# A retrieval search in a decoder block: seven weight tiles asked for ahead instead of four, and expert numbers computed before their gate weights

## The chip, the cores and the metric

The kernel runs on one core of one Trainium2 chip. The metric is the device time of one execution in microseconds (us); lower is better. The core has TensorE (PE, with its weight loads shown apart as PEld), VectorE (DVE), ScalarE (ACT), GpSimd (POOL) and SyncE (SP), which here issues most of the weight loads. Each engine runs its own list of instructions in a fixed order and waits on semaphores for the others; the DMA queues do the same.

## The reference, cut to what matters

512 tokens of width 1024 pass three attention-like mixers with gates and an output projection (`x`), and then a retrieval of experts, `peer_ffn`:

```
q  = h @ w_q                                  # 8 heads, two halves of 128 each
s1 = q[..., 0, :] . keys1 ; s2 = q[..., 1, :] . keys2      # 128 scores per half
v1, i1 = top_k(s1, 16) ; v2, i2 = top_k(s2, 16)
sv, si = top_k(all sums v1 + v2, 16)
experts = i1[si // 16] * 128 + i2[si % 16]    # the expert numbers
gates   = softmax(sv)                         # the gate weights
a   = h . u[experts]                          # 128 rows of u for each token
out = (gelu(a) * gates) . v[experts]          # 128 rows of v for each token
```

`u` and `v` hold 16384 rows of 1024 floats. The arithmetic of the kernel is 32-bit.

## The kernel before, in words

The tokens form four blocks of 128. `mixers(0)` computes the mixers for block 0, and `mixers(1)` those for blocks 1 to 3 together. While `mixers(1)` runs, a generator called `beside()` weaves in block 0's retrieval: the search, the numbers and weights, and then the rows of `u` and `v` that block 0's tokens picked ("tokens in rows": each row is gathered by an indirect DMA on POOL and multiplied on DVE). A function `pump`, called at each weight load of `mixers(1)`, moves `beside()` on by some credit. Blocks 2 and 3 are later done with dense matrix products over all experts, and block 1 in rows again beside them.

The order of instructions on each engine up to the end of the second search is not the order of the code. A scheduler with its own model of time builds it when the kernel is compiled: any edit moves instructions on every engine behind it. After the second search the order of POOL, DVE and PE is that of the code.

What the change touches lies in `beside()`:

- `search` for block 0 has 16 products on PE (line 766: `mm<-aT,...`), one for each head and half, each with a query weight tile of 512 KB from `w_pq`. `fetch` gives each its buffer: three slices of the idle tensor `mg1` and one buffer `raw`, four in turn. A tile is asked for when the code comes to its product, and its DMA waits until the product that used the buffer before is over.
- Per head, PE then does the scores (line 774), ACT copies them (line 777), and DVE finds the top 16 (lines 731 to 735).
- `weigh` computes the gate weights: a difference on DVE (line 801, tile `ex`), an exponential on ACT (line 804), a sum, a reciprocal and a product on DVE (810, 811, 813, tile `gate`).
- `numbers_of` computes the expert numbers `eidx` (DVE, up to line 869) and the tokens times norm factors, `h2n`, in tile `own` (DVE, line 872). Each gather (line 908) needs `eidx`, each row product (line 929, `scr<-row,own`) needs a landed row and `own`.

Other names in the rows: `rsy` (POOL, line 210) is the power -1/2 behind the norm of attention heads and waits for DVE's `rsv` (line 209), which needs DVE's sums of squares `hss` (line 351), which need ACT's squares of a finished PE product (line 350). `wlo` (DVE, line 138) is the low part of a weight tile that is split in two for exactness; PE's products of `mixers(1)` (lines 152 to 154) need it. `w_skvf`, `w_nat`, `w_o` and `w_out` are weights of the mixers. `qT`, `ohi` and `olo` are buffers of the attention: its queries, and the high and low part of its output.

## Time and profile before

| | us |
|---|---|
| median of 3 runs | 1552.13 |
| the runs | 1544.93, 1552.13, 1552.81 |
| the profiled execution, its own time | 1548.8 |
| its span (first to last instruction) | 1547.0 |
| PE busy | 1498.3 (97%) |
| DVE busy | 1419.4 (92%) |
| ACT busy | 812.4 (53%) |
| POOL busy | 778.1 (50%) |

The span is the profiler's, from the first to the last instruction, and 1.8 us lie around it. Block 0's search stands between 177 and 221 us of the span; its rows and `mixers(1)` fill the time to about 640 us; the second search ends near 760 us. Matmuls are pipelined and their ends are modelled, so the busy time of PE in a stretch is an upper bound of its work.

### The profile page before, as it was taken

How to read it: one execution, taken by the hardware profiler on the slowest of the kernel's cores; microseconds unless marked ns; L12 is line 12 of the kernel's file. 1: busy time of each engine (PE TensorE's matmuls, PEld its weight loads, DVE VectorE, ACT ScalarE, POOL GpSimd, SP SyncE). 2: the span in 40 equal slices, each digit the busy share in tenths (PEclk: the TensorE clock that was granted, in tenths of full speed). 3: DMA queues.
4: the chain of work that ended last, by engine and by line, in shares of the span. 5: the costliest groups of instructions: out<-in, count | busy, mean ns of one | idle time of the engine just before them, and what ended most of it. 6: DMA issues, size and time to landing. Idle time of an engine off the chain costs nothing.

```text
span 1547.0 us, 27092 instructions
## 1 busy us (share of the span) xinstructions
PE 1498.3 (97%) x9411; PEld 1360.5 (88%) x9411; DVE 1419.4 (92%) x2673; ACT 812.4 (53%) x1806; POOL 778.1 (50%) x642
## 2 busy tenths in 40 slices
PE   8999999999999989999999999999999999999998
PEld 7999899997897989999888887788888888888887
DVE  6689488989999999999999999899999999999998
ACT  7778346646345533352225899545444544544543
POOL 1101016767667456877445666545554544555451
PEclk9999999999998999999999999999999999999999
DMA  8688657998999898986998999999999999999995
GB/s 325 207 289 300 246 174 280 338 362 302 360 367 325 293 356 317 352 310 232 327 365 329 393 395 384 373 397 398 401 410 403 408 410 404 411 410 410 410 410 209
DMA packets 180125, 533.48 MB, mean 345 GB/s; under 512 B 17660, under 2 KB 48148, under 8 KB 179988
## 3 DMA queue, kind: packets, MB, share of 16 engines
q0 software_dynamic: 73728, 268.47, 45.9%
q1 hardware_dynamic: 96180, 227.54, 40.1%
q10 hardware_dynamic: 10080, 35.75, 5.8%
q8 instruction: 74, 1.21, 0.3%
q14 instruction: 63, 0.52, 0.1%
HBM read 516.99 MB, written 14.69 MB: 344 GB/s over the span
## 4 chain that ended last, share of the span: by engine, by line
PE 52%; issue 14%; DMA 11%; POOL 9%; DVE 9%; ACT 4%; POOLq 0%; DVEq 0%; SPq 0%; ACTq 0%
PE mm L153 9%; PE mm L152 9%; PE mm L154 9%; POOL row L908 9%; PE mm L1078 5%; DMA row<-in_peer_v_dram,eidx 4%; DMA row<-in_peer_u_dram,eidx 3%; PE sc L1078 3%; DVE wlo L138 2%; DMA gd<-st 2%; PE mm L766 2%; DVE o L1144 2%; DVE scr L929 1%; PE tp L384 1%; PE sc L506 1%
## 5 line engine op out<-in xcount | busy, mean ns | idle before, releaser
L908 POOL DMA_INDIRECT row<-in_peer_v_dram,eidx x256 | 322.2, 1258 | 298.3 <-DVE two L942 175.5
L908 POOL DMA_INDIRECT row<-in_peer_u_dram,eidx x256 | 315.4, 1232 | 219.8 <-DVE scr L929 115.8
L138 DVE TENSOR_TENSOR wlo<-raw,whi 128x1024 fp32r<-128x1024 f32 (+1 forms) x228 | 277.2, 1220 | 21.7 <-ACT whi L123 17.5
L942 DVE SCALAR_TENSOR_TENSOR two<-row,acts,two 128x1024 f32<-128x1024 f32 x197 | 252.6, 1282 | 5.3 <-DMA row<-in_peer_v_dram,eidx 3.1
L123 ACT CAST whi<-raw 128x1024 fp32r<-128x1024 f32 x146 | 152.2, 1050 | 119.2 <-PE mm L153 75.4
L929 DVE SCALAR_TENSOR_TENSOR scr<-row,own 128x1024 bf16<-128x1024 f32 x128 | 156.2, 1220 | 7.1 <-DMA row<-in_peer_u_dram,eidx 6.4
L929 DVE SCALAR_TENSOR_TENSOR scr<-row,two 128x1024 bf16<-128x1024 f32 x115 | 139.5, 1213 | 3.8 <-DMA row<-in_peer_u_dram,eidx 2.9
L210 POOL TENSOR_TENSOR rsy<-rsv,mhalf 128x4 f32<-128x4 f32 (+5 forms) x25 | 37.8, 1515 | 177.2 <-DVE rsv L209 176.3
L1212 ACT CAST ah<-ga 128x256 fp32r<-128x256 f32 x116 | 47.1, 407 | 150.2 <-PE tp L153 125.0
L152 PE MATMUL mm<-hhi,whi 128*128 128x384 f32 x320 | 110.8, 346 | 1.8 <-ACT hhi L244 1.4
L153 PE MATMUL mm<-hlo,whi 128*128 128x384 f32 x320 | 110.7, 346 | 0.0
L154 PE MATMUL mm<-hhi,wlo 128*128 128x384 f32 x320 | 109.9, 343 | 0.0
L152 PE MATMUL mm<-whi,hhi 128*128 128x256 f32 (+1 forms) x360 | 103.6, 290 | 2.7 <-ACT hhi L681 1.9
L1214 ACT CAST whi<-raw 128x1024 fp32r<-128x1024 f32 x96 | 100.3, 1047 | 9.5 <-DMA raw<-in_peer_v_dram 4.6
L153 PE MATMUL mm<-wlo,hhi 128*128 128x256 f32 (+1 forms) x360 | 102.7, 286 | 1.3 <-DVE wlo L138 1.3
L153 PE MATMUL sc<-wlo,ah 128*128 128x512 f32 x256 | 101.2, 395 | 2.5 <-DVE wlo L138 2.5
L152 PE MATMUL sc<-whi,ah 128*128 128x512 f32 x256 | 100.8, 394 | 1.3 <-ACT whi L1214 1.2
L154 PE MATMUL mm<-whi,hlo 128*128 128x256 f32 (+1 forms) x360 | 102.0, 285 | 0.0
L154 PE MATMUL sc<-whi,al 128*128 128x512 f32 x256 | 101.2, 395 | 0.0
L153 PE MATMUL tp<-wlo,ah 128*128 128x512 f32 x256 | 101.1, 395 | 0.0
L152 PE MATMUL tp<-whi,ah 128*128 128x512 f32 x256 | 101.0, 395 | 0.0
L154 PE MATMUL tp<-whi,al 128*128 128x512 f32 x256 | 100.6, 393 | 0.0
(332 smaller groups left out, 4478.2 us busy)
## 6 DMA issues: line engine op xcount, KB each, us to landing
raw<-in_peer_v_dram SPq DMA_DIRECT2D x96, 512.0 KB
hhi<-in_uT_dram ACTq DMA_DIRECT2D x68, 512.0 KB
raw<-in_w_tr_dram SPq DMA_DIRECT2D x48, 512.0 KB
raw<-in_w_nat_dram SPq DMA_DIRECT2D x40, 512.0 KB
last<-in_peer_v_dram SPq DMA_DIRECT2D x32, 512.0 KB
hhi<-in_uT_dram SPq DMA_DIRECT2D x26, 512.0 KB
raw<-in_w_o_dram SPq DMA_DIRECT2D x24, 512.0 KB
gd<-st SPq DMA_DIRECT2D x24, 512.0 KB
```

The lines of the kernel that those rows point to most:

```text
L123: ins = (cast or A.copy)(hi[:, :n * w], raw[:, :n * w])
L138: V.tensor_sub(lo, raw, hi.bitcast(F32))
L152: PE.matmul(ps, lh, rh, start=first, stop=False)
L153: PE.matmul(ps, lh, rl, start=False, stop=False)
L154: PE.matmul(ps, ll, rh, start=False, stop=last)
L210: G.tensor_tensor(y, v, mhalf[:, :n], op=OP.pow)
L908: ins = G.indirect_dma_start(out=r, out_offset=None, in_=t["peer_" + tab], in_offset=bass.IndirectOffsetOnAxis(ap=eidx[b][:, j:j + 1], axi ...
L929: V.scalar_tensor_tensor(scr, r, 1.0, two[0] if b else h2n[b], op0=OP.mult, op1=OP.mult, accum_out=acts[b][:, c]))
L942: V.scalar_tensor_tensor(two[0], r, acts[b][:, c], two[0], op0=OP.mult, op1=OP.add))
L1078: PE.matmul(ps[:, :TD], w[:, dc], h2f[dc], start=dc == 0, stop=dc == KC - 1)
L1212: A.copy(ah, a)
L1214: A.copy(hi, raw)
```

## The change

`fetch` now has seven buffers: to the three slices of `mg1` and `raw` come the buffers `qT`, `ohi` and `olo`, which nothing uses between the end of `mixers(0)` and the first queries and outputs of `mixers(1)`. It asks for tile i+6 when tile i is taken, so seven are asked for at the start. And `numbers_of` now comes ahead of `weigh`; two orders are pinned with `follow` (an edge for the scheduler without a semaphore): `own` and the first difference of the weights stand behind the cast to `eidx` on DVE.

```diff
-    def weigh(pool, f, g):
+    def follow(ins, after):
+        if after:
+            tc.add_manual_dep(ins.ins, after[-1], mybir.DependencyInfo(
+                mybir.DependencyClass.NoSync, mybir.DependencyReason.DATA), reason="behind the numbers")
+
+    def weigh(pool, f, g, after=()):
...
-        V.tensor_sub(ex, f.best, f.best[:, :, :, 0:1].to_broadcast([128, nb, PH, TOPK]))
+        follow(V.tensor_sub(ex, f.best, f.best[:, :, :, 0:1].to_broadcast([128, nb, PH, TOPK])), after)
...
-    def numbers_of(pool, f, lb, b, iota_k):
+    def numbers_of(pool, f, lb, b, iota_k, done=None):
...
-        V.tensor_copy(eidx[b], e[0])
+        ins = V.tensor_copy(eidx[b], e[0])
+        if done is not None:
+            done.append(ins.ins.name)
...
-        V.scalar_tensor_tensor(h2n[b], x1[b], rstd[:, b:b + 1], g2r, op0=OP.mult, op1=OP.mult)
+        follow(V.scalar_tensor_tensor(h2n[b], x1[b], rstd[:, b:b + 1], g2r, op0=OP.mult, op1=OP.mult), done)
...
-            lent, turns = by_token(wide("mg1", BIG)), [0]
+            lent = by_token(wide("mg1", BIG))
+            slots = [lent[:, i] for i in range(BIG)] + [qq.tile([128, D], F32, tag="raw", name="raw", bufs=1)]
+            slots += [pp.tile([128, 4, BIG * 128], F32, tag=tag, name="raw", bufs=1).rearrange("p a b -> p (a b)")[:, :D]
+                      for tag in ("qT", "ohi", "olo")]
+            asked, taken = [0], [0]
 
             def fetch(src, n):
-                i = turns[0] % (BIG + 1)
-                turns[0] += 1
-                raw = lent[:, i] if i < BIG else qq.tile([128, D], F32, tag="raw", name="raw", bufs=1)
-                fill(raw, src, n)
-                return raw
+                i = taken[0]
+                taken[0] += 1
+                while asked[0] < min(i + len(slots), 2 * PH):
+                    fill(slots[asked[0] % len(slots)], t["w_pq"][asked[0]], n)
+                    asked[0] += 1
+                return slots[i % len(slots)]
...
-            yield from weigh(pool, f, 0)
-            yield from numbers_of(pool, f, 0, 0, iota_k)
+            numbered = []
+            yield from numbers_of(pool, f, 0, 0, iota_k, numbered)
+            yield from weigh(pool, f, 0, numbered)
```

Three places of the compiled order bear on the prediction. In the rows a name is a tile, `<-` its sources, and xN counts equal rows; the changed kernel's lines stand 5 to 7 higher there (908 is 915, 929 is 936, 872 is 879).

The first is SP's list of loads around the start of the search, before (`mg1_2400` is `mg1`, `raw_2445` the buffer `raw`):

```order
L117 DMA raw_2340<-in_w_out_dram 128x1024
L117 DMA mg1_2400<-in_w_pq_dram 128x1024 x2
L117 DMA raw_2346<-in_w_out_dram 128x1024
L117 DMA mg1_2400<-in_w_pq_dram 128x1024
L758 DMA keys_2401<-in_keysT_dram 128x256
L758 DMA keys_2432<-in_keysT_dram 128x256
L117 DMA raw_2445<-in_w_pq_dram 128x1024
L117 DMA raw_2699<-in_w_skvf_dram 128x1056
L117 DMA raw_2891<-in_w_skvf_dram 128x1056
L117 DMA raw_3044<-in_w_nat_dram 128x1024
L117 DMA mg1_2400<-in_w_pq_dram 128x1024
```

The same stretch of SP now (`raw_2401` is the buffer `raw`, `raw_2403` lies in `ohi`, `raw_2404` in `olo`; the load into `qT` stands 13 rows further up, ahead of the last load of `w_o`):

```order
L117 DMA mg1_2400<-in_w_pq_dram 128x1024 x2
L117 DMA raw_2346<-in_w_out_dram 128x1024
L117 DMA mg1_2400<-in_w_pq_dram 128x1024
L117 DMA raw_2403<-in_w_pq_dram 128x1024
L117 DMA raw_2404<-in_w_pq_dram 128x1024
L758 DMA keys_2405<-in_keysT_dram 128x256
L117 DMA raw_2401<-in_w_pq_dram 128x1024
L758 DMA keys_2442<-in_keysT_dram 128x256
L117 DMA raw_2704<-in_w_skvf_dram 128x1056
L117 DMA raw_2885<-in_w_skvf_dram 128x1056
L117 DMA raw_3041<-in_w_nat_dram 128x1024
L117 DMA mg1_2400<-in_w_pq_dram 128x1024
```

Seven loads of `w_pq` now stand ahead of `w_skvf`, where four stood; the rows after the first four tiles alternate with `w_nat` as before.

The second is POOL's list from the first head norms of `mixers(1)`, before (`rsy` is the norm, `row` a gathered row of `u`):

```order
L210 TENSOR_TENSOR rsy<-rsv,mhalf 128x6
L210 TENSOR_TENSOR rsy<-rsv,mhalf 128x12
L908 DMA row<-in_peer_u_dram,eidx_212 128x1024 x6
L210 TENSOR_TENSOR rsy<-rsv,mhalf 128x12
L908 DMA row<-in_peer_u_dram,eidx_212 128x1024 x9
L210 TENSOR_TENSOR rsy<-rsv,mhalf 128x12
L908 DMA row<-in_peer_u_dram,eidx_212 128x1024 x7
```

And POOL now:

```order
L210 TENSOR_TENSOR rsy<-rsv,mhalf 128x6
L210 TENSOR_TENSOR rsy<-rsv,mhalf 128x12 x2
L915 DMA row<-in_peer_u_dram,eidx_212 128x1024 x14
L210 TENSOR_TENSOR rsy<-rsv,mhalf 128x12
L915 DMA row<-in_peer_u_dram,eidx_212 128x1024 x7
```

The second norm of 12 heads' sums has moved from behind the first six gathers to ahead of all of them.

The third is DVE's list from the last load split ahead of the first rows, before:

```order
L138 TENSOR_TENSOR wlo<-raw,whi 128x1024
L209 SCALAR_TENSOR_TENSOR rsv<-hss,eps 128x12
L929 SCALAR_TENSOR_TENSOR scr,acts_213<-row,own 128x1024 x2
L481 MEMSET qn 128x12
L483 TENSOR_SCALAR qn<-cum 128x12
L929 SCALAR_TENSOR_TENSOR scr,acts_213<-row,own 128x1024
L138 TENSOR_TENSOR wlo<-raw,whi 128x1024 x2
```

The cast to `eidx` stands five rows above this list: behind it came two pairs of `hss` and `wlo`, the second of which opens the list. The same place of DVE now (`own` and three of the four DVE instructions of the weights have come between the cast and this list, beside the two pairs):

```order
L138 TENSOR_TENSOR wlo<-raw,whi 128x1024
L209 SCALAR_TENSOR_TENSOR rsv<-hss,eps 128x12
L818 TENSOR_TENSOR gate_216<-ex,gden 128x8x16
L481 MEMSET qn 128x12
L483 TENSOR_SCALAR qn<-cum 128x12
L936 SCALAR_TENSOR_TENSOR scr,acts_213<-row,own 128x1024
L138 TENSOR_TENSOR wlo<-raw,whi 128x1024
L936 SCALAR_TENSOR_TENSOR scr,acts_213<-row,own 128x1024
```

The `wlo` that stood behind three rows stands behind one. On ACT the weights' exponential, which stood among the copies of the `w_skvf` product, now stands ahead of the last squares that this `rsv` needs, with a table load of its own; the later table load ahead of the attention's first exponential is gone.

## The prediction, and how it was worked out

> **What bounds the kernel now.** I read the page's shares and slices first, then the chain of work that ended last, then busy time by stage, and then the lists of PE, DVE, POOL and SP around block 0's search.

> ```profile
> span 1547.0 us, 27092 instructions
> PE 1498.3 (97%) x9411; PEld 1360.5 (88%) x9411; DVE 1419.4 (92%) x2673; ACT 812.4 (53%) x1806; POOL 778.1 (50%) x642
> PE 52%; issue 14%; DMA 11%; POOL 9%; DVE 9%; ACT 4%; POOLq 0%; DVEq 0%; SPq 0%; ACTq 0%
> 250.00:475.00 225.00, 220.68 (x1519) 201.88 (x1518) 208.82 (x392) 123.54 (x312) 159.69 (x120) 1.00 0.95 348
> 475.00:640.00 165.00, 152.78 (x956) 145.48 (x955) 157.80 (x213) 72.06 (x145) 105.39 (x76) 0.94 0.91 323
> 640.00:760.00 120.00, 120.00 (x672) 113.70 (x671) 119.39 (x623) 41.95 (x74) 84.83 (x87) 1.00 0.81 294
> ```

> PE and DVE share the bound; the last three rows give, after the length, the busy time of PE, PEld, DVE, ACT, POOL, then the granted clock. From 250 to 475 us DVE is idle 225 - 208.82 = 16.2 us and PE at most 4.3: there PE's stream leads and DVE has room. From 475 to 640 both have gaps (12.2 and 7.2 us) and the clock drops; from 640 to 760 DVE is full. So time saved on PE at 213 us can reach the end if PE stays ahead up to 640.

> The search itself is paced by PE, and PE waits in it for tiles:

> ```profile
> 177.08 0.39 PE L766 MATMUL mm<-aT,mg 128*128 128x128 f32 x2
> 188.71 3.84 PE L766 MATMUL mm<-aT,mg 128*128 128x128 f32 x32 [1.31 <-DMA mg<-in_w_pq_dram]
> 193.62 2.05 PE L766 MATMUL mm<-aT,raw 128*128 128x128 f32 x16 [1.07 <-DMA raw<-in_w_pq_dram]
> 195.51 0.61 PE L774 MATMUL sc<-keys,qp 128*128 128x128 f32 x4
> 196.31 0.91 PE L766 MATMUL mm<-aT,mg 128*128 128x128 f32 x6 [0.19 <-DMA mg<-in_w_pq_dram]
> 212.38 0.37 PE L152 MATMUL mm<-whi,hhi 128*128 128x264 f32 x1
> ```

> The brackets are the idle time ahead of a row and what ended it: 1.31 + 1.07 + 0.19 = 2.57 us in the 35.3 us from 177.08 to 212.38, where PE goes over to the mixers.

> **Part 1: seven tiles ahead.** No instruction is added; the 16 loads of 512 KB are issued earlier by SP.

> ```profile
> 158.85 0.42 SPq L117 DMA_DIRECT2D mg<-in_w_pq_dram  x1
> 172.41 0.42 SPq L117 DMA_DIRECT2D raw<-in_w_pq_dram  x1
> 180.96 0.33 SPq L117 DMA_DIRECT2D mg<-in_w_pq_dram  x1
> 161.45 3.72 PE L326 MATMUL mm<-raw,own 128*128 128x256 f32 x16 [0.33 <-ACT own L678]
> L153 PE MATMUL mm<-wlo,ohi x16: 275/279/283, 152.7 to 159.9; 128*128 128x256 f32 x16
> 162.00:171.00 9.00, 8.31 (x40) 7.09 (x39) 0.84 (x2) 1.61 (x5) 0.00 (x0) 1.00 0.25 102
> 177.00:192.00 15.00, 13.69 (x123) 13.50 (x122) 10.34 (x50) 6.99 (x18) 2.17 (x9) 1.00 0.85 314
> ```

> Before, three tiles are asked for by 158.85, the fourth at 172.41 and the fifth only at 180.96, when the first buffer is read. Now `ohi` and `olo` are free when PE's last product with them ends, about 160.2, and their loads stand ahead of the `keys` on SP, so they land in the stretch from 162 to 171, where the queues carry 102 GB/s (the last two figures of a row: share of the DMA engines, GB/s). `qT`'s load stands ahead of the last `w_o` and `w_out` loads on SP and delays each by its own length: at the 314 GB/s of 177 to 192, 0.52 MB take 1.7 us. The first `w_out` product (161.45) waits for ACT, not for its weights, so I cost that at nothing; if that cover were gone it costs up to 1.7.

> From the eighth tile on, a tile is asked for when PE leaves its buffer, about 181 for the first, and is needed seven products later. A product of 16 rows' matmuls takes 2.05 us by the row at 193.62, so that is 14 us, in which the queues move 4.4 MB at 314 GB/s: eight tiles' worth, for three or four tiles of `w_pq` and four of `w_nat` asked for meanwhile. So the 2.57 us go, whole; the bounds are 0 (the loads between eat the lead) and 2.57, and I take 2.57. PE then reaches `mixers(1)` at 209.8, and DVE, which waits for the scores, ends its search as much earlier.

> **Part 2: numbers before weights, on DVE.**

> ```profile
> 220.70 0.29 DVE L801 TENSOR_TENSOR ex<-best 128x128 f32<-128x128 f32 x1
> 223.10 0.28 DVE L810 TENSOR_REDUCE gden<-ex 128x8 f32<-128x128 f32 x1
> 223.77 0.19 DVE L811 RECIPROCAL gden<-gden 128x8 f32<-128x8 f32 x1
> 225.50 0.41 DVE L813 TENSOR_TENSOR gate<-ex,gden 128x128 f32<-128x128 f32 x1
> 225.82 1.28 DVE L872 SCALAR_TENSOR_TENSOR own<-mg,rstd,g2r 128x1024 f32<-128x1024 f32 x1
> 241.11 0.23 DVE L869 CAST eidx<-e 128x128 int32<-128x128 f32 x1
> 244.31 0.17 DVE L209 SCALAR_TENSOR_TENSOR rsv<-hss,eps 128x12 f32<-128x12 f32 x1
> 249.53 1.23 DVE L929 SCALAR_TENSOR_TENSOR scr<-row,own 128x1024 bf16<-128x1024 f32 x1 [5.06 <-DMA row<-in_peer_u_dram,eidx]
> 254.59 2.35 DVE L138 TENSOR_TENSOR wlo<-raw,whi 128x1024 fp32r<-128x1024 f32 x2
> ```

> Five instructions leave the way to `eidx`: 0.29 + 0.28 + 0.19 + 0.41 + 1.28 = 2.45 us, about 2 without the overlaps of neighbours. With part 1 the cast, 241.11 before, comes 2.57 + 2 = 4.5 us earlier, about 236.6. By itself that brings the gathers forward as much. But the order of POOL has changed too.

> ```profile
> 234.72 2.44 POOL L210 TENSOR_TENSOR rsy<-rsv,mhalf 128x12 f32<-128x12 f32 x1 [7.74 <-DVE rsv L209]
> 242.34 1.58 POOL L908 DMA_INDIRECT row<-in_peer_u_dram,eidx  x1 [5.18 <-ACT sq L350]
> 250.21 2.71 POOL L210 TENSOR_TENSOR rsy<-rsv,mhalf 128x12 f32<-128x12 f32 x1
> 221.34 0.40 ACT L804 ACTIVATE ex<-ex,rstd 128x128 f32<-128x128 f32 x1
> 224.17 1.28 ACT L439 ACT_TABLE_LOAD   x1
> 255.86 0.39 PE L153 MATMUL mm<-wlo,hhi 128*128 128x256 f32 x1 [1.28 <-DVE wlo L138]
> ```

> **Part 3: the gathers behind the second norm.** Before, `rsv` of 244.31 waits on POOL behind six gathers until 250.21. Now all gathers stand behind that norm. `rsv` hangs on PE's product and ACT's squares: 2.57 earlier at best, 241.7. Ahead of these squares ACT now has the weights' exponential and its table load, 0.40 + 1.28 = 1.7 us, so 243.4 at worst. The norm then takes 2.44 to 2.71 us with 0.2 ahead of and behind it: the first gather starts between 244.6 and 246.6, against 242.34. It comes 2.3 to 4.2 us later, though its numbers are 4.5 us earlier.

> DVE began the first row 249.53 - 242.34 = 7.2 us after its gather's start, so now at 251.8 to 253.8, and stands idle from about 242 on. Behind that row in its list stands the `wlo` for which PE waited 1.28 us before. It ends 1.23 + 1.2 us after the row's start, the 1.2 being half the pair of 2.35 at 254.59: 254.2 to 256.2, instead of 255.8. PE is ready for it at 255.86 - 1.28 - 2.57 = 252.0. So PE waits 2.2 to 4.2 us there, and goes on 1.7 us earlier to 0.3 later than before. I take the middle, 0.7 earlier: of 2.57 us gained in the search 1.9 go back. The terms in one line: -2.57 (tiles) + 1.9 (row and `wlo`) = -0.7.

> [...]

> The rows start 2.3 to 4.2 us later on DVE. I cost that at nothing behind this place: the 16.2 us idle on DVE up to 475 cover it, and the rows that stand ahead of the attention's later steps in DVE's list are fewer or the same. Without that cover it is up to 4.2 us in the full stretch up to 760. `weigh`'s last product on DVE (0.41) falls into the wait for the first row; the gate weights are read only after all 128 rows of `u`. The table load is one that stood later and goes there.

> The sum holds for the profiled execution: 1548.8 - 0.7 = 1548.1. That execution is 3.3 us under the median of the three runs, 1552.13, by which it would be 1551.4; I start from the middle of the two, 1550.5, and predict **1550**. The three runs differ by 7.9 us, 0.5%, which is about what a measurement of this kernel can tell from no change.

> **The rivals.** *PE's clock falls at the new wait (slower).* PE would stand 2.2 to 4.2 us in one piece. A wait like that has been seen in this trace:

> ```profile
> 482.67 0.44 PE L384 MATMUL tp<-cst,p 128*128 128x128 f32 x2 [2.12 <-ACT p L547]
> 480.00:485.00 5.00, 2.21 (x14) 1.74 (x13) 5.00 (x11) 3.30 (x9) 3.93 (x3) 0.87 1.00 354
> 485.00:490.00 5.00, 4.19 (x15) 3.02 (x15) 4.96 (x12) 2.45 (x7) 4.19 (x4) 0.50 0.94 308
> 490.00:495.00 5.00, 4.96 (x21) 4.24 (x20) 4.78 (x8) 1.90 (x4) 4.09 (x4) 0.61 0.87 300
> ```

> PE idled 2.8 of 5 us and ran at 0.50 and 0.61 afterwards: 0.13 x 5 + 0.50 x 5 + 0.39 x 5 = 5.1 us of lost clock. The shorter waits in the search left it at 1.00. From about 2.8 us of idle on it decides: -0.7 + 5.1 = +4.4, some 1555; with the wait at its upper bound and the late rows uncovered, 0.3 + 5.1 + 4.2 = +9.6, 1560. [...] Chance 0.22.

> *The order is kinder than I read it (faster).* The row lands sooner than 7.2 us, since weight loads share the queues less, and the gain of 2.57 stays; and the altered order around 480, with a row or two fewer ahead of the window attention's last steps in DVE's list, spares the clock drop there: -2.57 - 5.1 = -7.7, some 1543. That the gap at 480 is made of row products between short attention steps speaks for it; that as many matrix products as before are left to fill it speaks against. Chance 0.22.

> *The change doesn't do what it says.* SP's waits hold the extra loads back, or the queues do, and the search waits as before: then only part 3 is left, +1.9, some 1552. The idle queues from 162 to 171 speak against it. Chance 0.08.

> **How the numbers follow.** My forecast, a search without waits whose gain is mostly given back, has 0.48: 1547 to 1552 from the two starting points with its bounds. The range reaches to both clock cases, with the runs' own half spread of 4 us at each end cut to what leaves 2 in 10 out: 1541 to 1559. Faster by over 0.5% (under 1544.4) is most of the kind case and a share of the forecast through the runs' spread: 0.15 + 0.05 = 0.20. Slower by over 0.5% (over 1559.9) is the far end of the clock case and something not seen: 0.07 + 0.05 = 0.12. Within: 0.68.

> **What would show it.** Part 1: no idle time of PE for `w_pq` and a search of 32.7 us on PE. Part 2: `eidx` near 236.6. Part 3: the norm of 12 ahead of the first gather, that at 244.6 to 246.6, DVE idle 9 us or more for the first row, PE waiting for `wlo` near 252. The clock in 250 to 275 tells the slow rival, that in 480 to 495 the fast one. I am wrong if PE runs through 252 to 256, or if the stretches behind 475 differ by more than 5 us.

## The result, and the profile after

The changed kernel takes 1560.96 us (median of 8 runs, 1555.07 to 1566.08) against 1552.12 for the kernel before (8 runs beside it, 1544.93 to 1554.93): a ratio of 1.0060, with a 95% interval of 1.0039 to 1.0082. It is slower, by more than the prediction's range (1541 to 1559) allowed.

The page of the kernel after, its first two lines:

```profile
span 1558.2 us, 27098 instructions
PE 1504.3 (97%) x9411; PEld 1364.2 (88%) x9411; DVE 1418.9 (91%) x2673; ACT 812.5 (52%) x1806; POOL 782.3 (50%) x642
```

The span is 11.2 us longer with the same instructions on PE, DVE, ACT and POOL. PE is busy 6.0 us longer, which is about what the clock lost (44.4 us at half speed instead of 30.7, half of the difference is 6.8); the rest is waits. Busy time by stage, in the columns of the prediction's rows:

```profile
177.00:213.00 36.00, 36.00 (x315) 35.74 (x314) 24.09 (x150) 11.39 (x33) 5.38 (x25) 1.00 0.68 247
250.00:475.00 225.00, 221.40 (x1514) 202.93 (x1513) 202.68 (x382) 121.40 (x303) 161.85 (x119) 0.99 0.93 343
475.00:640.00 165.00, 148.32 (x929) 140.10 (x928) 153.37 (x204) 68.97 (x144) 98.68 (x72) 0.92 0.88 309
640.00:760.00 120.00, 118.31 (x679) 112.91 (x678) 116.52 (x627) 46.05 (x79) 88.38 (x90) 1.00 0.84 299
```

From 475 to 640 us PE's idle time has grown from 12.2 to 16.7 us, DVE's from 7.2 to 11.6, and the clock has gone from 0.94 to 0.92.

Setting the starts of the same PE products in the two traces against each other tells where PE falls behind. "Clock" is half of the time for which the granted clock stood at 0.5, against the kernel before.

| stretch (time of before), us | PE later by, us | of which clock |
|---|---|---|
| 150 to 177, ahead of the search | +1.6 | +1.7 |
| 177 to 212, the search | -3.3 | 0 |
| 212 to 262, start of `mixers(1)` | +5.4 | +1.7 |
| 262 to 470 | +0.6 | +1.7 |
| 470 to 642 | +7.8 | +3.4 |
| 642 to the end | -1.2 | 0 |

So the search gained what was predicted, and two places gave back four times as much: the start of `mixers(1)`, which the prediction worked out, and a stretch 260 us behind the edit, which it had costed at nothing. (The first row of the table is no work of the change; the last section says why.) PE's list in the kernel after, first the search, then its waits of 0.2 us or more up to 262 us:

```profile
179.04 0.39 PE L766 MATMUL mm<-aT,mg 128*128 128x128 f32 x2
208.62 2.17 PE L766 MATMUL mm<-aT,mg 128*128 128x128 f32 x18
210.55 0.37 PE L152 MATMUL mm<-whi,hhi 128*128 128x264 f32 x1
...
227.86 0.33 PE L377 MATMUL tg<-cst,qn 128*128 128x128 f32 x1 [1.79 <-ACT qn L363]
229.35 0.55 PE L152 MATMUL mm<-whi,hhi 128*128 128x256 f32 x1 [0.20 <-ACT sq L350]
247.62 0.39 PE L152 MATMUL mm<-whi,hhi 128*128 128x256 f32 x1 [0.63 <-ACT sq L350]
259.70 0.39 PE L153 MATMUL mm<-wlo,hhi 128*128 128x256 f32 x1 [0.44 <-DVE wlo L138]
```

No product from 179.04 to 210.55 waits for `w_pq`; the search takes 31.5 us instead of 35.3. The new wait stands at 227.86, and the one forecast near 252 is missing. POOL and DVE around it:

```profile
223.57 3.62 POOL L210 TENSOR_TENSOR rsy<-rsv,mhalf 128x6 f32<-128x6 f32 x1 [5.51 <-DVE rsv L209]
249.92 2.27 POOL L210 TENSOR_TENSOR rsy<-rsv,mhalf 128x12 f32<-128x12 f32 x1 [9.09 <-DVE rsv L209]
252.37 1.15 POOL L915 DMA_INDIRECT row<-in_peer_u_dram,eidx  x1 [0.18 <-PE tg L377]
...
229.23 0.07 DVE L487 MEMSET qn<- 128x12 f32 x1 [1.60 <-PE tg L377]
242.03 0.23 DVE L874 CAST eidx<-e 128x128 int32<-128x128 f32 x1
249.76 0.41 DVE L818 TENSOR_TENSOR gate<-ex,gden 128x128 f32<-128x128 f32 x1
257.27 1.23 DVE L936 SCALAR_TENSOR_TENSOR scr<-row,own 128x1024 bf16<-128x1024 f32 x1 [4.69 <-DMA row<-in_peer_u_dram,eidx]
```

The first row is the norm of 6 heads' sums, which took 1.78 us before:

```profile
225.20 1.78 POOL L210 TENSOR_TENSOR rsy<-rsv,mhalf 128x6 f32<-128x6 f32 x1 [6.53 <-DVE rsv L209]
```

The expert numbers are ready at 242.03, later than before (241.11), and the gathers start at 252.37 instead of 242.34.

### The profile page after: what moved, and what is told of

It reads as the page before. It is cut to its first block, busy times and chain, and to the rows that moved or that the text cites. A ratio compares the mean times of both kernels' runs of the same rounds, so it can differ in the third digit from the quotient of the medians.

```text
span 1558.2 us, 27098 instructions
## 1 busy us (share of the span) xinstructions
PE 1504.3 (97%) x9411; PEld 1364.2 (88%) x9411; DVE 1418.9 (91%) x2673; ACT 812.5 (52%) x1806; POOL 782.3 (50%) x642
## 4 chain that ended last, share of the span: by engine, by line
PE 47%; DVE 16%; issue 14%; POOL 10%; DMA 7%; ACT 5%; POOLq 0%; DVEq 0%; SPq 0%; another core or an unknown queue 0%; ACTq 0%
POOL row L915 8%; PE mm L154 7%; PE mm L153 7%; PE mm L152 7%; PE mm L1091 5%; PE sc L1091 3%; DVE two L949 3%; DVE wlo L138 2%; DMA row<-in_peer_u_dram,eidx 2%; DMA row<-in_peer_v_dram,eidx 2%; DMA gd<-st 2%; PE sc L153 2%; PE sc L154 2%; PE tp L152 2%; PE tp L153 2%
## 5 line engine op out<-in xcount | busy, mean ns | idle before, releaser
L138 DVE TENSOR_TENSOR wlo<-raw,whi 128x1024 fp32r<-128x1024 f32 (+1 forms) x228 | 277.4, 1220 | 22.4 <-ACT whi L123 19.5
L210 POOL TENSOR_TENSOR rsy<-rsv,mhalf 128x4 f32<-128x4 f32 (+5 forms) x25 | 41.8, 1676 | 188.8 <-DVE rsv L209 188.0
L152 PE MATMUL mm<-hhi,whi 128*128 128x384 f32 x320 | 110.6, 346 | 1.8 <-ACT hhi L244 1.4
L153 PE MATMUL mm<-hlo,whi 128*128 128x384 f32 x320 | 110.7, 346 | 0.0
L152 PE MATMUL mm<-whi,hhi 128*128 128x256 f32 (+1 forms) x360 | 104.9, 294 | 2.4 <-DVE mg L693 0.8
L153 PE MATMUL mm<-wlo,hhi 128*128 128x256 f32 (+1 forms) x360 | 103.3, 288 | 0.4 <-DVE wlo L138 0.4
L153 PE MATMUL sc<-wlo,ah 128*128 128x512 f32 x256 | 101.2, 395 | 2.1 <-DVE wlo L138 2.1
L152 PE MATMUL sc<-whi,ah 128*128 128x512 f32 x256 | 100.8, 394 | 1.3 <-ACT whi L1227 1.2
L152 PE MATMUL tp<-whi,ah 128*128 128x512 f32 x256 | 101.1, 395 | 0.0
L153 PE MATMUL tp<-wlo,ah 128*128 128x512 f32 x256 | 101.0, 395 | 0.0
```

The lines of the kernel that those rows point to most:

```text
L138: V.tensor_sub(lo, raw, hi.bitcast(F32))
L152: PE.matmul(ps, lh, rh, start=first, stop=False)
L153: PE.matmul(ps, lh, rl, start=False, stop=False)
L210: G.tensor_tensor(y, v, mhalf[:, :n], op=OP.pow)
```

## The experiments

Three theories stood at the start, and the expectations call them A, B and C. A: *numbers first* is at fault (the wait at 227.86, late rows). B: *pieces of time at half clock* are at fault, which any small shift can bring or spare. C: the *tiles* are at fault (loads asked for early hold up those of `w_out`). Four came up on the way. D: it is the *new order* that the scheduler makes on all engines behind any edit. H: the clock falls for want of work on PE, and work without use would hold it up. N, the small norm on POOL runs longer while DVE does long products beside it. M, the buffers of the gathered rows lie in the space of the tiles that `weigh` uses, so that the first gather waits for the last reader of these tiles. "Pinned" means that the instructions of PE, DVE, ACT and POOL from the start of `mixers(1)` to the end of the second search are tied to a given order by edges without semaphores; the orders are packed as lists of numbers and not printed here:

```
for row in ROWS_OF.values():              # PE, DVE, ACT, POOL: numbers of the instructions in the wanted order
    for x, y in zip(row, row[1:]):
        tc.add_manual_dep(traced[y], x, NoSync)
```

| kernel | what | order | median, us (runs) | ratio to before, 95% |
|---|---|---|---|---|
| after | both parts | new | 1560.96 (8) | 1.0060 (1.0039 to 1.0082) |
| e1_tiles_only | seven tiles | new | 1556.01 (12) | 1.0034 (1.0015 to 1.0053) |
| e2_order_only | numbers first | new | 1564.32 (7) | 1.0071 (1.0046 to 1.0096) |
| e4_exp_first | both, exponential ahead | new | 1563.64 (6) | 1.0079 (1.0055 to 1.0103) |
| e6_order_of_tiles | four tiles, weights first: the order of e1 alone | pinned to e1 | 1558.81 (6) | 1.0058 (1.0042 to 1.0074) |
| e5_tiles_pinned | seven tiles | pinned to before | 1548.80 (12) | 0.9987 (0.9975 to 0.9999) |
| e7_numbers_pinned | tiles, weights and `own` behind numbers | pinned | 1551.54 (12) | 1.0015 (1.0002 to 1.0029) |
| e8_own_stays | tiles, weights behind numbers | pinned | 1552.24 (12) | 1.0013 (0.9995 to 1.0031) |
| e9_ex_apart | tiles, gate behind numbers, other tile | pinned | 1549.24 (10) | 0.9993 (0.9976 to 1.0010) |
| e10_norm_beside | e5, long products beside the norm | pinned | 1546.57 (1) | a single run |
| e11_busy | e5 with extra PE products | pinned | 1548.39 (12) | 0.9984 (0.9967 to 1.0001) |

### Each part alone

```diff
 # e1_tiles_only: the change without its last hunk
-            numbered = []
-            yield from numbers_of(pool, f, 0, 0, iota_k, numbered)
-            yield from weigh(pool, f, 0, numbered)
+            yield from weigh(pool, f, 0)
+            yield from numbers_of(pool, f, 0, 0, iota_k)
 # e2_order_only: the change with the fetch of before (four buffers in turn)
```

> Seven tiles ahead, with the weights ahead of the numbers as in the kernel before; the order of gathers and norms on POOL is that of before. Theory A (the order of numbers and weights costs, the tiles gain): PE's search takes 31.5 to 32 us as in the changed kernel, the norm of 6 stays under 2 us, PE is 2.5 to 3.5 us earlier at 260 us, and the time is 1546 to 1550. Theory B (the loss is half-speed clock windows that any small shift can bring or spare, whatever the part): the search is as short, but the time lies anywhere from 1543 to 1562, by the half-speed time between 475 and 640 us. Theory C (the loads asked for early delay the w_out loads and so PE at 155 us): PE is 1.6 us later at 160 us, the time 1550 to 1552.

> Four tiles ahead as in the kernel before, numbers ahead of weights as in the changed one. Theory A: PE waits 2 to 3 us for the query weights as before, the norm of 6 takes over 3 us and the first gather starts after 250 us; the whole loss of the changed kernel and the gain of the tiles on top, 1560 to 1567. Theory B: anywhere from 1545 to 1565, by the half-speed time. Theory C: no loss ahead of 176 us, time as before, 1550 to 1554.

Each part alone is slower than before. e2 has the time and the signs that A gave it (norm of 6 3.62 us, first gather at 255.36 us), but it has a new order too. For e1, A asked for 1546 to 1550, and 1556.0 came; C's sign, PE 1.6 us later at 160 us, is there, but e6 below shows the same without the tiles. In e1 the search gains 3.2 us and every engine keeps the order of before from the end of the search up to 386 us; nothing up to there is late. Then the lists differ, and PE waits for DVE. The place in DVE's list, in the kernel before and in e1 (`mg`, gated output, is what PE's next product hangs on; `scr<-row,own` are row products of block 0):

```profile
386.47 0.75 DVE L542 TENSOR_REDUCE nm<-sc 128x1 f32<-128x256 f32 x2
387.13 1.21 DVE L929 SCALAR_TENSOR_TENSOR scr<-row,own 128x1024 bf16<-128x1024 f32 x1
388.27 0.55 DVE L616 SCALAR_TENSOR_TENSOR mg<-g,mm 128x384 f32<-128x384 f32 x1
```

```profile
385.39 0.42 DVE L542 TENSOR_REDUCE nm<-sc 128x1 f32<-128x256 f32 x1
385.73 1.22 DVE L936 SCALAR_TENSOR_TENSOR scr<-row,own 128x1024 bf16<-128x1024 f32 x1
386.87 0.42 DVE L542 TENSOR_REDUCE nm<-sc 128x1 f32<-128x256 f32 x1
387.21 1.21 DVE L936 SCALAR_TENSOR_TENSOR scr<-row,own 128x1024 bf16<-128x1024 f32 x1
388.42 0.55 DVE L616 SCALAR_TENSOR_TENSOR mg<-g,mm 128x384 f32<-128x384 f32 x1
389.02 0.44 PE L152 MATMUL mm<-ohi,whi 128*128 128x384 f32 x1 [2.24 <-DVE mg L616]
```

Two row products of 1.2 us now stand ahead of `mg` where one stood. DVE was ahead by 1.1 us and uses that on a row product; PE, which also came earlier, waits 2.24 us (before, its longest wait near this place is 1.01 us, for ACT). By 500 us e1 has lost 7.1 us against before. That is no collision of loads. It spoke for the new order, but e1 holds tiles and order together.

### The order without the tiles, the tiles without the order

```diff
 # e5_tiles_pinned: e1, pinned to the order of before
 # e6_order_of_tiles: the kernel before, pinned to the order of e1
```

> Seven tiles ahead, weights ahead of numbers, and every instruction of PE, DVE, ACT and POOL from the second mixers to the end of the second search pinned to the order that the kernel before has there. Theory D (the tiles do gain their 3.2 us; what loses is the new order that the scheduler makes behind 384 us): PE keeps its lead of some 3 us from 212 to 640 us, no new wait near 388 us, and the time is 1545 to 1549, 3 to 8 below the seven tiles alone (1556.0). Theory B (a shift of the same work against the clock's windows loses by itself): 1551 to 1558 as with the tiles alone. If the early loads themselves cost (clock at 154 us), the time is 1.6 higher than by D, 1547 to 1551.

> The kernel before, with four tiles ahead, and the same instructions pinned to the order that the scheduler made for seven tiles. Theory D: PE waits for tiles in its search as before, then loses behind 384 us as with the tiles alone (a wait of 2 us for DVE near 389 us, some 5 us by 500 us): 1555 to 1560, slower than before by 0.3 to 0.7%. Theory B: no shift, so no loss, 1549 to 1552.

These two tell D from B and C: B asked for at least 1551 from e5 and at most 1552 from e6. C asked for PE 1.6 us later at 160 us, which e5, with seven tiles, does not show and e6, with four, does. With seven tiles and the order of before, PE leaves the search 3.3 us earlier and is still at least as much earlier at 700 us; the kernel is faster by 0.13% (0.01 to 0.25). With four tiles, no other instruction and no other load, the order of e1 alone costs 0.58% (0.42 to 0.74), and PE has the same wait of 2.24 us for `mg` (at 391.42). The clock is a small part of that: (1 - granted clock) x time is 17.1 us in the runs of e6 and 14.4 in those of before beside them, 2.7 more, while the mean time is 9.2 longer. The waits of PE over 0.9 us from 470 to 500 us, in before, e6 and after:

```profile
482.67 0.44 PE L384 MATMUL tp<-cst,p 128*128 128x128 f32 x2 [2.12 <-ACT p L547]
```

```profile
487.61 0.70 PE L584 MATMUL sc<-mkT,qT 128*128 128x256 f32 x2 [0.95 <-ACT qT L388]
492.75 1.03 PE L415 MATMUL tp<-cst,o 128*128 128x128 f32 x4 [3.56 <-DVE o L411]
```

```profile
489.71 0.69 PE L384 MATMUL tp<-cst,p 128*128 128x128 f32 x2 [4.29 <-ACT p L547]
493.17 1.06 PE L377 MATMUL tg<-cst,qn 128*128 128x128 f32 x2 [1.49 <-ACT qn L363]
```

The wait of 2.12 us has become 3.56 in e6 and 4.29 in after, in the short attention steps between DVE's rows. Runs of e6 and e1 differ by the tiles alone: 1558.8 and 1556.0, 2.8 us apart, where the tiles are worth 3.3.

### A gentler variant of the change

```diff
 # e4_exp_first: the change, with the weights' difference and exponential ahead of the numbers again
-            yield from numbers_of(pool, f, 0, 0, iota_k, numbered)
-            yield from weigh(pool, f, 0, numbered)
+            yield from weigh(pool, f, 0, [])      # calls numbers_of behind its exponential
```

> The changed kernel, but the weights' difference and exponential stand ahead of the numbers as in the kernel before; only the sum, the reciprocal and the product stand behind them. ACT loads no table between the squares of mixers(1), and POOL has six gathers ahead of the second norm of 12 again. Theory A: of the 5.7 us that PE loses between 220 and 260 us some 3 are spared (1.7 of ACT, the rest from the gathers), the norm of 6 may still be slowed beside the DVE products; 1548 to 1556. Theory B: no relation with the order, 1545 to 1565 by the half-speed time. If the norm of 6 is what costs, PE still idles about 2 us near 228 us and the clock falls there, and the time stays above 1555.

The table load of ACT and the exponential stand where they stood before, and the kernel is as slow (1.0079; A had asked for 1548 to 1556). Its start is good: the norm of 6 takes 2.70 us, PE waits 0.49 us for it with no piece at half clock, and at 262 us PE is 1.4 us earlier than before. But it got yet another order, with 20.5 us at half clock in the stretch from 375.9 us on, and by 384 us it is 9 us late. What the exponential is worth can't be read from its time. That is why the next ones are pinned.

### Numbers first, with the order held

```diff
 # e7_numbers_pinned: e5, with own, ex, gden, gate on DVE moved behind the cast and the third rsv,
 #                    and the exponential moved on ACT behind the copies of kT
 # e8_own_stays: as e7, own left in its place
 # e9_ex_apart: e5, with gden and gate moved behind them; and the weights in another tile:
-        ex = pool.tile([128, nb, PH, TOPK], F32, name="ex")
+        ex = acts[0]...
```

> Seven tiles and the order of before as in the pinned kernel, but the weights and the own product moved on DVE behind the numbers and behind the third norm's rsv, and the weights' exponential on ACT behind the kT copies: both parts of the change without the scheduler's other moves. Theory N (the norm of 6 on POOL is held while DVE runs the numbers' products with two operands in SBUF): the norm of 6 takes over 3 us against 1.8, PE idles some 2 us near 225 us and its clock may fall there; 2 to 5 us slower than with own left in place (e8), about 1549 to 1553. Without N: the first gather starts at 237 to 239, PE does not wait near 252, 1544 to 1548.

> As e7, but the own product stays on DVE where it stands before, ahead of the numbers' first large product; only the four instructions of the weights move. Theory N: the norm of 6 takes 1.8 to 2.2 us again, PE does not idle near 225 us, and the time is 1545 to 1549, 2 to 5 below e7. Without N: e7 and e8 within 1 us of each other.

> Seven tiles and the order of before, with only the weights' sum, reciprocal and product moved on DVE behind the numbers and the third norm's rsv, as in e8; but the exponentials lie in the tile of the row sums, not in the pool whose space the rows take over. Theory M (the first gather waits for the last reader of that pool, since its rows take the space: gate end + 1.0 us in e7, e8 and the changed kernel): the first gather starts 1.0 us after the cast of eidx again, before the weights' product ends, PE does not wait for the third norm near 250 us, and the time is that of the pinned tiles, 1546 to 1549. Without M (the gathers were late for the order of POOL or for the loads): the first gather still starts 1 us after the weights' product, some 7 us after the cast, and PE waits 5 us near 253 us, 1551 to 1553.

First N. The norm of 6 takes 1.56 us in e7 (N asked for over 3) and 1.57 in e8, and e8 is 0.7 us above e7, not 2 to 5 below: in both, only 0.67 us of a long DVE product lie beside the norm, so they do not test N. That the time of e7 lies in N's range has another cause, M. The cast, `gate` and first gather in e5, then in e7, where the first row is what DVE waits for ahead of the cast:

```profile
221.20 0.41 DVE L828 TENSOR_TENSOR gate<-ex,gden 128x128 f32<-128x128 f32 x1
236.05 0.23 DVE L884 CAST eidx<-e 128x128 int32<-128x128 f32 x1
237.28 1.15 POOL L925 DMA_INDIRECT row<-in_peer_u_dram,eidx  x1 [4.43 <-PE tp L387]
242.06 1.23 DVE L946 SCALAR_TENSOR_TENSOR scr<-row,own 128x1024 bf16<-128x1024 f32 x1 [1.87 <-DMA row<-in_peer_u_dram,eidx]
```

```profile
229.73 0.42 DVE L361 TENSOR_REDUCE hss<-sq 128x4 f32<-128x256 f32 x1 [1.11 <-ACT sq L360]
235.09 0.23 DVE L884 CAST eidx<-e 128x128 int32<-128x128 f32 x1
240.43 0.40 DVE L828 TENSOR_TENSOR gate<-ex,gden 128x128 f32<-128x128 f32 x1
241.84 1.15 POOL L925 DMA_INDIRECT row<-in_peer_u_dram,eidx  x1 [11.09 <-PE mm L164]
253.49 0.42 PE L387 MATMUL tg<-cst,qn 128*66 128x128 f32 x1 [5.53 <-ACT qn L373]
```

In e7 the gather is 4.6 us later. The cast is 1.0 us earlier, but so is the whole execution, from ahead of the search on: with the same PE products behind the search set against each other, the cast stands at 241.1 us of the time of before in both, as it does in before itself. So moving five instructions out of the way of the numbers brought them forward by nothing; DVE waits for ACT's squares instead, as it does for 0.73 us in before:

```profile
235.76 0.42 DVE L351 TENSOR_REDUCE hss<-sq 128x4 f32<-128x256 f32 x1 [0.73 <-ACT sq L350]
```

The first gather starts 1.0 us after the end of `gate` in e7, in e8 as well (243.39 + 0.40, gather at 244.79), and in e5 1.0 us after the end of the cast. (In after, against what the expectation of e9 says, it starts 2.2 us behind `gate`: there the norm ahead of it in POOL's list held it.) The name behind the arrow is of no help: it is another one each time. The six gathers then stand ahead of the norm that PE waits for, 5.5 us. In e9 the weights lie in another tile, and `gate` is as late as in e7:

```profile
237.68 0.23 DVE L884 CAST eidx<-e 128x128 int32<-128x128 f32 x1
238.91 2.20 POOL L925 DMA_INDIRECT row<-in_peer_u_dram,eidx  x1 [4.57 <-ACT whi L133]
242.12 0.42 DVE L828 TENSOR_TENSOR gate<-acts,gden 128x128 f32<-128x128 f32 x1
```

The gather starts 1.0 us after the cast again, 3.2 us ahead of `gate`, and the wait of 5.5 us is gone. So M is shown: the rows' buffers take the space of the tile `ex`, and the gathers wait until the product `gate` has read it. "Numbers first" without that move cannot bring a gather forward. With it, the kernel is no faster than e5: 0.9993 and 0.9987 (1549.24 us, just above M's 1546 to 1549). PE waits 2.21 us for `wlo` at 253.14 and the clock goes to half once, against a wait of 1.81 and no such piece in e5.

### The norm on POOL

```diff
 # e10_norm_beside: e5, on DVE one wlo moved from ahead of the rsv of 6 to just behind it, and own up to behind that
```

> Seven tiles and the order of before, but on DVE the rsv of the norm of 6 comes ahead of the wlo before it, so that the norm on POOL runs beside two long DVE products in a row with both operands in SBUF (wlo 1.2 us, own 1.3 us), as in the changed kernel it ran beside three. Theory N (such products hold POOL off): the norm takes 2.3 us or more, against 1.77 in the pinned kernel and 1.56 to 1.57 in e7 and e8. Without N: 1.3 to 1.8 us.

```profile
221.83 2.25 POOL L220 TENSOR_TENSOR rsy<-rsv,mhalf 128x6 f32<-128x6 f32 x1 [5.39 <-DVE rsv L219]
```

The norm of 6 took 2.25 us, with 1.06 us of `wlo` and 0.85 of `own` on DVE beside it. That is just under what N asked for and well over the other side's 1.3 to 1.8. The same instruction took 1.57 us beside 0.64 of `own` (e9), 1.77 beside 1.15 (e5) and 3.62 in after, beside 1.05 of `wlo` and 2.2 of the two long products `hot` of the numbers. In these four runs it was the longer, the more of the long two-input products of DVE lay beside it (0.64, 1.15, 1.91 and 3.25 us); N holds in kind. A longer norm also lies beside more of them by itself, and each kernel has one trace, so the size per product is not settled.

### Half speed of PE

```diff
 # e11_busy: e5, with 29 products of the unit matrix put into PE's six longest waits from 477 to 955 us
+            ins = self.pe.matmul(out[:, :128], self.eye, self.eye, start=True, stop=True)
```

> The pinned kernel with 29 products of the unit matrix with itself on PE, 0.22 us each, ahead of the six products before which PE waits longest between 477 and 955 us (2.1, 1.4, 1.9, 1.4, 1.0 and 2.0 us); they go to the bank that the waiting product overwrites. Theory H (the clock falls to half for 3.4 us after a window of 3.4 us in which PE was busy for less than about 0.55 of the time): the half-speed time between 470 and 960 us goes from 17 to 20 us to at most 4, and the kernel gains 5 to 8 us, 1540 to 1543. Without H: the products cost or change nothing, the half-speed stretches stay, 1548 to 1551.

The expectation was missed: 1548.4 us, as e5. The pieces at half speed between 470 and 960 us went from 20.5 us in e5 to 13.7, not to 4. Two stretches of e5, then the same of e11:

```profile
470.00:500.00 30.00, 26.39 (x141) 22.65 (x140) 29.09 (x57) 16.08 (x41) 23.64 (x17) 0.83 0.92 321
560.00:642.00 82.00, 72.72 (x495) 69.54 (x495) 77.47 (x128) 32.14 (x63) 53.71 (x40) 0.96 0.91 325
```

```profile
470.00:500.00 30.00, 27.23 (x159) 23.53 (x159) 29.10 (x56) 16.53 (x46) 23.77 (x19) 0.89 0.94 334
560.00:642.00 82.00, 74.45 (x522) 71.16 (x521) 78.17 (x122) 31.73 (x62) 52.68 (x36) 0.98 0.90 320
```

The clock rose from 0.83 to 0.89 and from 0.96 to 0.98, and from 470 to 642 us e11 gained nothing on e5 (0.7 us longer by the same PE products). DVE is busy 97% and 95% there. In the short attention steps PE waits for DVE and ACT (2.12 us for ACT in before, 3.56 for DVE in e6); that a faster PE only waits longer there fits, but no run shows it apart.

## Why the prediction was wrong

**Part 1 held.** The search has no wait for tiles, takes 31.5 us (32.7 forecast; one more group of scores fell behind its end), and PE keeps its 3.3 us where the order is left alone (e5, to 700 us). Of the time 2.0 us go, with 0.2 to 3.9 by the interval. The load of `qT` ahead of the `w_out` tiles cost nothing that e5 shows.

**The step that failed most is "I cost that at nothing behind this place".** The prediction looked for the price of later rows in DVE's idle time up to 475 us, and found room. What costs is not the rows' start but where they and the attention's steps stand in the lists. In e7, which has both parts with the order otherwise held, PE loses 6 us at the wait near 253, but from 262 to 642 us only 0.4 more against before; after loses 8.4 there. By time, both parts cost 0.15% with the order held (e7) and 0.60% without. The sentence about "the altered order around 480" was there, as a gain of 5.1 us in the fast rival only; it should have stood as a loss with the same weight. The order of e1 alone costs 0.58% (e6), some 9 us. After has another order than e1, and no run has that order with the code of before; that it costs as it does in e6 is read from e7 and from PE's waits for DVE and ACT. All five kernels with a newly made order are slower than before, by 0.3 to 0.8%; those pinned to the order of before and timed more than once lie between -0.2 and +0.2%.

**Part 2 failed.** The cast was to come at 236.6 and came at 242.03. The search gave its part, 0.8 us more than forecast. The second term, 2 us for five instructions that leave the way, is worth nothing where the order is held (e7): ACT's squares of PE's products are summed ahead of the numbers in DVE's list and hold it up there, and the prediction took DVE's own work for the bound. Another 2.0 us stood ahead of the search, most of it in a piece at half clock. The last 2.3 go with a wait that the prediction never looked at: the norm of 6 (3.62 instead of 1.78 us), for which PE stood 1.79 us. DVE waited 1.60 us for the same product to have read `qn`, which it clears ahead of the next steps of the numbers (229.23), and then the clock stood at 0.50 for 3.41 us (from 229.39). Together: 236.6 - 0.8 + 2 + 2.0 + 2.3 = 242.1.

**Part 3 had the right order and the wrong times.** The norm of 12 stands ahead of all gathers, as said, but it starts at 249.92 and the first gather at 252.37, not 244.6 to 246.6. A later `rsv` did that (249.68 against 241.7 to 243.4). And even without it the gather could not have come before `gate`, by M. From gather to row on DVE it took 4.9 us, not 7.2: the DMA queues carried 178 GB/s in that time, and 242 in before. Over the kernels of this case it went with that load: 4.5 to 4.9 us at 168 to 180 GB/s (4.8 in e5), 6.1 to 7.4 at 205 to 290. PE ran through 252 to 256, which the prediction itself had named as the sign of its error.

Yet up to here part 1's gain was given back, as forecast: without the clock, PE is 0.3 us later at 262 us (1.6 - 3.3 + 5.4, less 3.4 of clock) where -0.7 was said. The sum came out near by other waits than those in it, which is luck. (Its reading of the first rows has a slip that changes nothing: PE is idle *at least* 4.3 us from 250 to 475, not at most, since its busy time is an upper bound.)

**The slow rival was near in kind.** The clock did fall after a wait, but at 229 us after 1.79 us, not at 252 after 2.8. That it falls from about 2.8 us of idle on was the author's estimate from one stretch of before (480 to 485 us), and no run shows that point: in the traces the clock fell after single waits of 1.79 us (after, 227.86) and 2.12 us (before, 482.67), and after two of 1.05 and 0.73 us close together (after, 152.88 and 154.35; the last section). Over all runs, (1 - granted clock) x time is 14.1 us for before (70 runs) and 22.0 for after, 7.9 more, while the mean time rose by 10.4. Among runs of one kernel, 1 us more of it goes with 0.76 us of time. By that, some 6 of the 10.4 us go with the clock and 4 with waits alone. This is a correlation: e11 took 4.5 us of lost clock away (15.5 to 11.0) and won 0.2 us. How much of the loss of after is the clock's own, and how much the waits that bring it about, stays open.

## What to carry to other kernels

Where a scheduler makes the order from modelled times, an edit that shortens one stage can reorder everything behind it, and that order can cost more than the edit saves: time the edit with the order pinned to the old one, and the new order with the old code, before judging either. When an instruction is moved later, ask which buffers lie in the space that its tiles free; here the trace showed it as a start that follows the end of a reader by 1.0 us in e4, e7 and e8, not by the name it prints. And an instruction taken out of a list saves time only if the list is what the next step waits for. If the engine that is made faster feeds another that is full, as in e11, its clock or its gaps may be a sign and not a price.

## What the runs showed of the hardware

```profile
222.57:225.98 3.41, 3.41 (x30) 3.30 (x28) 3.41 (x11) 1.95 (x4) 2.41 (x1) 1.00 0.99 369
225.98:229.39 3.41, 1.12 (x5) 0.46 (x4) 1.78 (x6) 2.17 (x9) 1.21 (x1) 1.00 0.48 148
229.39:232.80 3.41, 3.41 (x16) 3.41 (x17) 2.38 (x8) 1.43 (x4) 0.00 (x0) 0.50 0.00 0
```

PE is busy 1.12 of 3.41 us, and the next piece holds 16 products instead of 30. In after a piece begins at 150.9 us, in before at 149.2. That of after holds two short gaps, 1.67 us busy, and the next ran at 0.50; in before a stretch just as idle lies across the edge of two pieces (149.2 to 152.6 and 152.6 to 156.0, 2.35 and 2.67 us busy), and the clock stayed at 1.00:

```profile
150.90:154.30 3.40, 1.67 (x13) 1.24 (x11) 3.40 (x6) 2.72 (x5) 0.00 (x0) 1.00 0.97 312
154.30:157.70 3.40, 3.35 (x16) 3.35 (x17) 1.41 (x3) 0.81 (x2) 0.00 (x0) 0.50 0.89 323
```

```profile
151.00:154.40 3.40, 1.62 (x12) 1.19 (x11) 3.40 (x6) 2.22 (x5) 0.00 (x0) 1.00 1.00 314
154.40:157.80 3.40, 3.40 (x31) 3.40 (x31) 2.39 (x5) 2.48 (x4) 0.00 (x0) 1.00 0.82 304
```

The 1.7 us of the first row of the table by stretches are thus not the change's: e6, with four tiles, has them too, and e5, with seven, has not.
